# Hybrid encoder trunk on one core: 1/rms of a phase's tokens by ScalarE's square root, VectorE's reciprocal and one Newton step

## Chip, core and metric

The kernel runs on one core of a Trainium2 chip. The core has TensorE (PE in the profile; its weight loads are PEld), VectorE (DVE), ScalarE (ACT), GpSimd (POOL) and SyncE (SP), each with its own instruction stream that runs in order; they wait for each other by semaphores. The metric is the device time of one execution in microseconds, as the median over runs.

## The reference

Two layers, each a token mixer (gated delta rule, pooling, retention) and a SwiGLU feed-forward network, on 512 tokens of 1024 channels in float32. Each of the two halves of a layer is wrapped in two RMS norms, one ahead of it and one behind it:

```python
def rms_norm(x, w):
    xf = x.astype(jnp.float32)
    y = xf * lax.rsqrt(jnp.mean(xf * xf, axis=-1, keepdims=True) + RMS_EPS) * w.astype(jnp.float32)
    return y.astype(x.dtype)

def reference(x, mix_pre_norm, ..., ffn_down):
    for l in range(DEPTH):
        h = rms_norm(x, mix_pre_norm[l])
        m = hybrid_mixer(h, w_in[l], ...)
        x = x + rms_norm(m, mix_post_norm[l])
        h = rms_norm(x, ffn_pre_norm[l])
        x = x + rms_norm(swiglu(h, ffn_gate[l], ffn_up[l], ffn_down[l]), ffn_post_norm[l])
    return x
```

The mixer's gates of the delta rule use a sigmoid (`beta`) and exponentials (the decay `g`); the other gates are sigmoids.

## The kernel before

Activations lie with channels on the 128 partitions and the 512 tokens along the free dimension, in eight tiles of 128x512. Every float32 product is made of three matmuls of rounded operands (`mm3`, lines 225 to 228): each operand is split into a high part, which ScalarE rounds, and a low part, which VectorE gets by subtracting (`split`, `split1`, lines 230 to 237). The names are `hh`/`hl` for the normed input, `wh`/`wl` for weights, `oh`/`ol` for a branch's input, `ah`/`al` for the feed-forward activation. Products go to PSUM tiles `pp` and `cx`, small ones to `fx`.

A norm takes these steps. ScalarE squares the tiles (`sq`, line 286), GpSimd adds them (`sqa`, line 293), TensorE sums over the partitions against a column of ones (`rms_tok`, line 271), so that each token's sum stands on a partition, in 2 or 4 columns. VectorE takes 1/sqrt there (`rms_tok` line 273 and `rsqrt`, lines 239 to 264: a start value from the exponent bits, then two polynomial steps; ten instructions in all, `rsv`, `rsi`, `rsy`, `rsa`, `rsb`). TensorE spreads the result over the partitions (`spread`, line 279), and others multiply by it. `rsqrt` is called in the mixer too, for other norms.

`mean_square` (line 320) is called 15 times. `begin` (line 361) calls it once at the very start, for the first layer's input. `hand_over` (line 399) joins two halves of the network, and runs four times. It makes the last output blocks of one half in two token halves of 256 (`produce`), norms each half (`accs`), adds it to the residual `xt` and splits the new operand (`step`: lines 332, 333, 232, 233, 286), and starts the first four products of the next half: three in `cx` banks (`group_step`) and a fourth in a `pp` bank (`alone`). The next half's own norm (`pre`) is spread while that runs (lines 463 to 469) and behind it (474 to 476). At the end of the kernel (lines 412 to 431) `hand_over` only finishes: the last spread is followed by lines 341 and 342 and the output's DMA.

At the start of a mixer `token_gates` (line 527) works out `beta` (sigmoid, 551), `e` (exp of the tokens' decay, 563), `ea` (exp of a layer constant, 565) and, through a chain of small VectorE instructions, `g`, whose sums TensorE makes at line 591. At the same time the pooling branch's operands `oh` are split (line 1014, which calls `split`) for the first branch product `pp<-oh,wh`.

ScalarE's functions come from tables, and where the table that is loaded lacks a function, an ACT_TABLE_LOAD stands ahead of the instruction. Copies and squares stand behind any of the loads. Before the change 24 loads stand on ScalarE: the first at the start, the others where sigmoid and exp take turns, eleven in the first mixer and twelve in the second.

The order of each engine's stream is set by a scheduler from the program order, priorities (`tc.high_priority`, lines 210 and 219) and its own estimate of each instruction. `tc.issue_after(ins)` keeps what is traced in its block behind `ins` on its engine. So an edit in one helper moves instructions elsewhere.

Of the kernel before, what the change touches and what calls it, by code (L numbers as in the profile page):

```python
# [9 lines left out]
F32 = mybir.dt.float32  # L10
F32R = mybir.dt.float32r
I32 = mybir.dt.int32
AF = mybir.ActivationFunctionType
ALU = mybir.AluOpType
# [121 lines left out]
def tile_hybrid(ctx: ExitStack, tc: tile.TileContext, x_in, consts, rot, rmask, vecs, wab, wi, wpl, wbr, wo, wgu, wd, out):  # L136
# [18 lines left out]
    one = cpool.tile([P, 1], F32, tag="one", name="one")  # L155
    V.memset(one0, 1.0)
    A.activation(out=one, in_=one0, func=AF.Copy)

    def cm(n):
        return kc[:, n * P : (n + 1) * P]  # L160
# [18 lines left out]
    def nm(s):  # L179
        uid[0] += 1  # L180
        return f"{s}_{uid[0]}"

    def psum(pool, tag):
        return pool.tile([P, S], F32, tag=tag, name=nm(tag))
# [10 lines left out]
    def psum_o():  # L195
        return psum(fx, "fx")
# [42 lines left out]
    def rsqrt(pool, v, n):  # L239

        def new(tag, bufs=2, dt=F32):
            return pool.tile([P, n], dt, tag=f"{tag}{n}", bufs=bufs, name=nm(tag))

        i = new("rsi", dt=I32)
        V.tensor_scalar(out=i, in0=v.bitcast(I32), scalar1=1, scalar2=None, op0=ALU.logical_shift_right)
        y = new("rsy", 4)
        V.tensor_scalar(out=y.bitcast(I32), in0=i, scalar1=-1.0, scalar2=1597463007.0, op0=ALU.mult, op1=ALU.add)
        a = new("rsa")  # L250
        V.tensor_tensor(out=a, in0=y, in1=y, op=ALU.mult)
        b = new("rsb")
        V.tensor_tensor(out=b, in0=a, in1=v, op=ALU.mult)
        a = new("rsa")
        V.scalar_tensor_tensor(out=a, in0=b, scalar=-3.4181694869972654, in1=b, op0=ALU.add, op1=ALU.mult)
        z = new("rsy", 4)
        V.scalar_tensor_tensor(out=z, in0=a, scalar=5.24672026895501, in1=y, op0=ALU.add, op1=ALU.mult)
        a = new("rsa")
        V.scalar_tensor_tensor(out=a, in0=z, scalar=-0.0625, in1=z, op0=ALU.mult, op1=ALU.mult)
        b = new("rsb")  # L260
        V.tensor_tensor(out=b, in0=a, in1=v, op=ALU.mult)
        y = new("rsy", 4)
        V.scalar_tensor_tensor(out=y, in0=b, scalar=1.5, in1=z, op0=ALU.add, op1=ALU.mult)
        return y

    def rms_tok(sqs, ps, scale, eps):

        n = sqs[0].shape[1] // P
        for t in range(n):
            for i, sq in enumerate(sqs):  # L270
                T.matmul(ps[:, t : t + 1], lhsT=sq[:, ts(t)], rhs=one, start=i == 0, stop=i == len(sqs) - 1)  # L271
        v = hpool.tile([P, n], F32, tag=f"rsv{n}", bufs=2, name=nm("rsv"))
        V.tensor_scalar(out=v, in0=ps[:, :n], scalar1=8 * scale, scalar2=8 * eps, op0=ALU.mult, op1=ALU.add)
        return rsqrt(hpool, v, n)

    def spread(r, ps):

# [41 lines left out]

    def mean_square(acc):  # L320

        return rms_tok(acc, psum_o(), 1.0 / D, RMS_EPS)

    def spread_new(r):
        ps = psum_f()
# [26 lines left out]
    def rest(gen):  # L352
        for _ in gen:
            pass
# [5 lines left out]

    def begin(pool, l, v0, srcs):

        z = pool.tile([P, S // 2], F32, tag="z", name="z")
        V.memset(z, 0.0)
        ps = psum_f()
        for _ in range(4):
            T.matmul(ps[:, 0 : S // 2], lhsT=z[:, 0:P], rhs=z, start=True, stop=True)
        n = 3 * P
        xs = [pool.tile([P, S], F32, tag="xt", bufs=KT, name=nm("xt")) for _ in range(KT)]
        raw, wh, wl = (pool.tile([P, KT * n], t, tag=a, name=a) for a, t in (("w", F32), ("wh", F32R), ("wl", F32R)))  # L370
        for k in range(KT):
            nc.sync.dma_start(out=xs[k], in_=x_in[k])
            nc.sync.dma_start(out=raw[:, k * n : (k + 1) * n], in_=srcs[0][k])
        nc.sync.dma_start(out=ident, in_=consts[:, 0:P])
        hs, rb = operands()
        pss = [psum_c() for _ in range(3)]
        for k in range(KT):
            split(xs[k], vec[:, l, v0 + k : v0 + k + 1], *hs[k])
            high = nc.cur_bb.bb.instructions[-2]
            sl = slice(k * n, (k + 1) * n)  # L380
            split1(raw[:, sl], wh[:, sl], wl[:, sl])
            for j, ps in enumerate(pss):
                at = slice(k * n + j * P, k * n + (j + 1) * P)
                mm3(ps, (wh[:, at], wl[:, at]), hs[k], k == 0, k == KT - 1)
        f = last_block(srcs[3], hs, pss)
        with tc.issue_after(high):
            acc = accumulate(pool, None, xs)
        some(f, 2)
        r = mean_square(acc)
        rest(f)  # L390
        f = last_block(srcs[4], hs, pss)
        some(f, 1)
        A.activation(out=rb, in_=spread_new(r), func=AF.Copy)
        last["rb"] = nc.cur_bb.bb.instructions[-1]
        rest(f)
        nc.sync.dma_start(out=kc, in_=consts[:, P:])
        return x_in, hs, rb, pss

    def hand_over(pool, l, v_post, xs, pairs, ms, produce, nxt):
# [2 lines left out]
        w = vec[:, l, v_post : v_post + KT]  # L402
        h0, h1 = HALVES
        accs = {}
        rest(produce(0, accs))
        p1 = produce(1, accs)
        some(p1, 2)
# [96 lines left out]
    def mixer(l, xd, hs, rb, firsts):  # L504
# [22 lines left out]
        def token_gates():  # L527
# [34 lines left out]
            e = tiny("e")  # L562
            A.activation(out=e, in_=nab, func=AF.Exp)
            ea = tiny("ea")
            A.activation(out=ea, in_=vec[:, l, V_ALOG : V_ALOG + 16], func=AF.Exp)
            den = tiny("den")
            V.tensor_scalar(out=den, in0=e, scalar1=2.0, scalar2=None, op0=ALU.add)
            V.reciprocal(out=den, in_=den)
# [873 lines left out]
```

## Time and profile before

| | |
|---|---|
| median of 3 runs | 1843.85 us (1843.64 to 1846.25) |
| the profiled execution | 1842.82 us |
| its span, first to last instruction | 1841.0 us |
| mean granted TensorE clock | 0.997 |
| PE busy | 1814.3 us (99%) |
| PEld busy | 1536.9 us (83%) |
| DVE busy | 1052.1 us (57%) |
| ACT busy | 711.3 us (39%) |
| POOL busy | 373.3 us (20%) |

A matmul's duration in the trace overlaps that of the next one, so TensorE's rate is read from the distance of starts: 256 columns follow each other by 0.12 us, 512 columns by 0.23 us. A wait in square brackets names what ended the idle time. Idle time of TensorE is what the kernel can still lose or win; idle time of the others costs nothing by itself.

### The profile page before, as it was taken

How to read it: one execution, taken by the hardware profiler on the slowest of the kernel's cores; microseconds unless marked ns; L12 is line 12 of the kernel's file. 1: busy time of each engine (PE TensorE's matmuls, PEld its weight loads, DVE VectorE, ACT ScalarE, POOL GpSimd, SP SyncE). 2: the span in 40 equal slices, each digit the busy share in tenths (PEclk: the TensorE clock that was granted, in tenths of full speed). 3: DMA queues.
4: the chain of work that ended last, by engine and by line, in shares of the span. 5: the costliest groups of instructions: out<-in, count | busy, mean ns of one | idle time of the engine just before them, and what ended most of it. 6: DMA issues, size and time to landing. Idle time of an engine off the chain costs nothing.

```text
span 1841.0 us, 25237 instructions
## 1 busy us (share of the span) xinstructions
PE 1814.3 (99%) x9528; PEld 1536.9 (83%) x9528; DVE 1052.1 (57%) x1998; ACT 711.3 (39%) x1272; POOL 373.3 (20%) x350
## 2 busy tenths in 40 slices
PE   9999999999999999999999999999999999999997
PEld 7777888888898888888987778888888988888887
DVE  7778766664457432444687787666644574324443
ACT  5553333333344333333445533333334443333331
POOL 2040211011233210221210402110121332102212
PEclk9999999999999999999999999999999999999998
DMA  5312212124325222222232221221343252323221
GB/s 186 118 59 94 75 61 83 58 81 137 103 81 183 101 94 100 95 94 102 81 127 94 89 82 64 72 72 47 103 138 117 73 178 92 103 92 100 95 92 47
DMA packets 65850, 177.74 MB, mean 97 GB/s; under 512 B 15424, under 2 KB 19648, under 8 KB 65728
## 3 DMA queue, kind: packets, MB, share of 16 engines
q1 hardware_dynamic: 58800, 173.04, 28.0%
q10 hardware_dynamic: 6928, 3.08, 0.6%
q8 instruction: 75, 1.23, 0.3%
q14 instruction: 47, 0.39, 0.1%
HBM read 167.18 MB, written 8.39 MB: 95 GB/s over the span
## 4 chain that ended last, share of the span: by engine, by line
PE 90%; DVE 7%; ACT 1%; issue 1%; DMA 0%; SPq 0%; POOL 0%; ACTq 0%; DVEq 0%
PE pp L226 26%; PE pp L228 26%; PE pp L227 26%; DVE ct L641 1%; DVE wl L237 1%; PE cx L227 1%; PE cx L226 1%; PE cx L228 1%; PE cx L849 1%; PE cx L932 1%; PE fx L271 1%; PE cx L942 1%; PE cx L834 1%; PE cx L521 1%; PE fx L521 1%
## 5 line engine op out<-in xcount | busy, mean ns | idle before, releaser
L226 PE MATMUL pp<-hh,wh 128*128 128x512 f32 (+1 forms) x1592 | 626.2, 393 | 0.0
L228 PE MATMUL pp<-hh,wl 128*128 128x512 f32 (+1 forms) x1592 | 616.9, 387 | 0.0
L227 PE MATMUL pp<-hl,wh 128*128 128x512 f32 (+1 forms) x1592 | 615.4, 387 | 0.0
L236 ACT ACTIVATE wh<-raw 128x512 fp32r<-128x512 f32 x570 | 355.0, 628 | 665.6 <-PE pp L227 609.8
L237 DVE TENSOR_TENSOR wl<-raw,wh 128x512 fp32r<-128x512 f32 x570 | 417.6, 738 | 264.4 <-ACT wh L236 254.7
L228 PEld LDWEIGHTS pp<-hh,wl 128*128 128x128 f32 x1592 | 299.0, 188 | 61.9 <-issue 0.7
L226 PEld LDWEIGHTS pp<-hh,wh 128*128 128x128 f32 x1592 | 299.3, 188 | 59.8 <-issue 1.0
L227 PEld LDWEIGHTS pp<-hl,wh 128*128 128x128 f32 x1592 | 299.4, 188 | 57.4
L226 PE MATMUL pp<-ah,wh 128*128 128x512 f32 (+1 forms) x376 | 134.7, 358 | 0.0
L227 PE MATMUL pp<-al,wh 128*128 128x512 f32 (+1 forms) x376 | 134.4, 357 | 0.0
L228 PE MATMUL pp<-ah,wl 128*128 128x512 f32 (+1 forms) x376 | 134.4, 357 | 0.0
L1309 POOL TENSOR_TENSOR gs<-gt,sg 128x512 f32<-128x512 f32 x44 | 56.7, 1288 | 314.0 <-ACT sg L1307 314.0
L1314 POOL TENSOR_TENSOR a<-gs,ut 128x512 f32<-128x512 f32 x44 | 70.5, 1602 | 130.1 <-DVE ut L1312 129.6
L293 POOL TENSOR_TENSOR sqa<-sqa,sq 128x256 f32<-128x256 f32 (+1 forms) x73 | 68.7, 941 | 107.4 <-ACT sq L286 88.1
L226 PEld LDWEIGHTS pp<-ah,wh 128*128 128x128 f32 x376 | 71.0, 189 | 10.5
L227 PEld LDWEIGHTS pp<-al,wh 128*128 128x128 f32 x376 | 71.1, 189 | 10.3
L228 PEld LDWEIGHTS pp<-ah,wl 128*128 128x128 f32 x376 | 71.0, 189 | 10.3
L237 DVE TENSOR_TENSOR al<-a,ah 128x512 fp32r<-128x512 f32 x44 | 31.3, 711 | 77.7 <-ACT ah L236 77.4
L226 PE MATMUL pp<-yh,wh 128*128 128x256 f32 (+1 forms) x224 | 67.1, 300 | 0.0
L228 PE MATMUL pp<-yh,wl 128*128 128x256 f32 (+1 forms) x224 | 66.8, 298 | 0.0
L227 PE MATMUL pp<-yl,wh 128*128 128x256 f32 (+1 forms) x224 | 66.8, 298 | 0.0
L1036 POOL TENSOR_TENSOR y<-y,ft 128x512 f32<-128x512 f32 x16 | 26.5, 1653 | 189.6 <-DVE ft L1035 173.1
(327 smaller groups left out, 2468.0 us busy)
## 6 DMA issues: line engine op xcount, KB each, us to landing
raw<-in_wi_dram SPq DMA_DIRECT2D x117, 512.0 KB
raw<-in_wgu_dram SPq DMA_DIRECT2D x88, 512.0 KB
raw<-in_wd_dram SPq DMA_DIRECT2D x44, 512.0 KB
raw<-in_wbr_dram SPq DMA_DIRECT2D x24, 512.0 KB
raw<-in_wo_dram SPq DMA_DIRECT2D x16, 512.0 KB
xd<-xt SPq DMA_DIRECT2D x24, 256.0 KB
xt<-xd SPq DMA_DIRECT2D x24, 256.0 KB
xt<-in_x_dram SPq DMA_DIRECT2D x16, 256.0 KB
```

The costliest lines, as they stand in the source:

```text
L226: T.matmul(ps, lhsT=w[0], rhs=m[0], start=start, stop=False)
L227: T.matmul(ps, lhsT=w[0], rhs=m[1], start=False, stop=False)
L228: T.matmul(ps, lhsT=w[1], rhs=m[0], start=False, stop=stop)
L236: A.activation(out=hi, in_=src, func=AF.Copy)
L237: V.tensor_tensor(out=lo, in0=src, in1=hi.bitcast(F32), op=ALU.subtract)
L271: T.matmul(ps[:, t : t + 1], lhsT=sq[:, ts(t)], rhs=one, start=i == 0, stop=i == len(sqs) - 1)
L293: G.tensor_tensor(out=t, in0=acc[0], in1=acc[1], op=ALU.add)
L521: T.transpose(ps[:, ts(t)], src[:, ts(t)], ident)
L641: V.scalar_tensor_tensor(out=a2, in0=u[:, j : j + S], scalar=tap(j), in1=a, op0=ALU.mult, op1=ALU.add)
L1036: G.tensor_tensor(out=ys[n], in0=ys[n], in1=t, op=ALU.add)
L1309: G.tensor_tensor(out=gs, in0=gt, in1=sg, op=ALU.mult)
L1314: G.tensor_tensor(out=a, in0=gs, in1=ut, op=ALU.mult)
```

## The change

`rms_tok` no longer calls `rsqrt`. ScalarE takes sqrt(scale*x + eps) from PSUM, VectorE takes the same sum's plain value `v`, the reciprocal of the root, and one Newton step of three instructions. That is one instruction on ScalarE and five on VectorE in place of ten on VectorE, 15 times.

Sqrt has a table of its own. `root_table` runs a Sqrt on one column so that the load stands early: at the start of `begin`, and at the start of each `hand_over`, there behind the ScalarE instruction that was traced last (`behind`). In `token_gates` the exponential `ea` is tied behind `e`. The other calls of `rsqrt` stay.

```diff
+    eps = cpool.tile([P, 1], F32, tag="eps", name="eps")
+    V.memset(eps, RMS_EPS)
...
+    def behind(engine):
+        return tc.issue_after(next(i for i in reversed(nc.cur_bb.bb.instructions) if i.engine == engine))
...
-    def rms_tok(sqs, ps, scale, eps):
+    def rms_tok(sqs, ps, scale):
...
-        v = hpool.tile([P, n], F32, tag=f"rsv{n}", bufs=2, name=nm("rsv"))
-        V.tensor_scalar(out=v, in0=ps[:, :n], scalar1=8 * scale, scalar2=8 * eps, op0=ALU.mult, op1=ALU.add)
-        return rsqrt(hpool, v, n)
+        q, v, y, z = (new(t) for t in ("rsq", "rsv", "rsy", "rsz"))
+        a, b = new("rsa", 1), new("rsb", 1)
+        A.activation(out=q, in_=ps[:, :n], func=AF.Sqrt, scale=scale, bias=eps)
+        V.tensor_scalar(out=v, in0=ps[:, :n], scalar1=scale, scalar2=RMS_EPS, op0=ALU.mult, op1=ALU.add)
+        V.reciprocal(out=y, in_=q)
+        V.scalar_tensor_tensor(out=a, in0=y, scalar=-0.5, in1=y, op0=ALU.mult, op1=ALU.mult)
+        V.tensor_tensor(out=b, in0=a, in1=v, op=ALU.mult)
+        V.scalar_tensor_tensor(out=z, in0=b, scalar=1.5, in1=y, op0=ALU.add, op1=ALU.mult)
+        return z
+
+    def root_table():
+        t = hpool.tile([P, 1], F32, tag="rst", name=nm("rst"))
+        A.activation(out=t, in_=one0, func=AF.Sqrt)
...
     def begin(pool, l, v0, srcs):
+        root_table()
...
     def hand_over(pool, l, v_post, xs, pairs, ms, produce, nxt):
...
+        with behind(A.engine):
+            root_table()
         rest(produce(0, accs))
...
-            A.activation(out=ea, in_=vec[:, l, V_ALOG : V_ALOG + 16], func=AF.Exp)
+            with behind(A.engine):
+                A.activation(out=ea, in_=vec[:, l, V_ALOG : V_ALOG + 16], func=AF.Exp)
```

The scheduler then sets other orders. Three places follow; line numbers of the changed kernel are larger by about 26 (split is 238 and 239, spread 301, `ea` 591, `oh` 238).

ScalarE at the very start: `one` is the column of ones, `hh` the first operand's high part. Before:

```order
L157 ACT_TABLE_LOAD
L157 ACTIVATE one<-one_79 128x1
L232 ACTIVATE hh_121<-xt_93,vec 128x512
L236 ACTIVATE wh<-w 128x384
L232 ACTIVATE hh_123<-xt_94,vec 128x512
```

After:

```order
L157 ACT_TABLE_LOAD
L157 ACTIVATE one<-one_79 128x1
L296 ACT_TABLE_LOAD
L296 ACTIVATE rst_88<-one_79 128x1
L238 ACTIVATE hh_125<-xt_97,vec 128x512
```

A load and a one-column root stand ahead of the first operand.

TensorE in the first `hand_over`, where `pre[0]`'s result `rsy` (after: `rsz`) is spread; `cx` are the three grouped products of the next half, `pp` the fourth. Before:

```order
L228 MATMUL cx_5223<-hh_5005,wl_5242 128x256
L226 MATMUL pp_5226<-hh_4999,wh_5358 128x256
L227 MATMUL pp_5226<-hl_5000,wh_5358 128x256
L228 MATMUL pp_5226<-hh_4999,wl_5359 128x256
L226 MATMUL cx_5221<-hh_5007,wh_5275 128x256
L226 MATMUL cx_5222<-hh_5007,wh_5282 128x256
L226 MATMUL cx_5223<-hh_5007,wh_5289 128x256
L226 MATMUL pp_5226<-hh_5001,wh_5358 128x256
L227 MATMUL pp_5226<-hl_5002,wh_5358 128x256
L279 MATMUL fx_5539<-ident,rsy_5429 128x128 x2
L227 MATMUL cx_5221<-hl_5008,wh_5275 128x256
```

After:

```order
L234 MATMUL cx_5213<-hh_4995,wl_5232 128x256
L232 MATMUL cx_5211<-hh_4997,wh_5265 128x256
L232 MATMUL cx_5212<-hh_4997,wh_5272 128x256
L232 MATMUL cx_5213<-hh_4997,wh_5279 128x256
L301 MATMUL fx_5513<-ident,rsz_5396 128x128
L233 MATMUL cx_5211<-hl_4998,wh_5265 128x256
```

The spread now comes in two parts, the first five `pp` matmuls earlier. The `pp` product is moved to the rear: 19 of its 24 matmuls follow the last `cx` matmul, where 12 did. The other two middle `hand_over`s read the same.

ScalarE in the second layer's `token_gates`: `beta` and the two `ft` are sigmoids, `e` and `ea` exponentials, `ct` and `oh` need no table of their own. Before (`ea`, with a load of its own, stands seven rows ahead of this piece):

```order
L551 ACT_TABLE_LOAD
L551 ACTIVATE beta_9032<-fx_9017 128x16
L975 ACTIVATE ft_8938<-ft_8936 128x512
L236 ACTIVATE wh_9303<-raw_9284 128x512
L975 ACTIVATE ft_8977<-ft_8975 128x512
L232 ACTIVATE oh_9088<-fx_9086,vec 128x512
L563 ACT_TABLE_LOAD
L563 ACTIVATE e_9038<-nab_9036 128x16
L638 ACTIVATE ct_9054<-ft_9051,vec 128x512
L232 ACTIVATE oh_9100<-fx_9098,vec 128x512
```

After:

```order
L576 ACT_TABLE_LOAD
L576 ACTIVATE beta_8968<-fx_8953 128x16
L1001 ACTIVATE ft_8874<-ft_8872 128x512
L242 ACTIVATE wh_9239<-raw_9220 128x512
L1001 ACTIVATE ft_8913<-ft_8911 128x512
L588 ACT_TABLE_LOAD
L588 ACTIVATE e_8974<-nab_8972 128x16
L591 ACTIVATE ea_8976<-vec 128x16
L664 ACTIVATE ct_8990<-ft_8987,vec 128x512
L238 ACTIVATE oh_9024<-fx_9022,vec 128x512
L238 ACTIVATE oh_9036<-fx_9034,vec 128x512
```

The first `oh` moves from ahead of the load to behind `ct`. In the first layer it already stood there before the change (load, `e`, `ct`, `oh`); there only `ea` comes in between `e` and `ct`.

In all, ScalarE has 30 table loads after the change: one more at the start, one more in each of the four `hand_over`s, one more at the first sigmoid of each of the two feed-forward networks, and one less for `ea`. None stands directly ahead of a norm's root.

## Rows read from the trace of the kernel before

**Rows 1.** The page: engine totals, and the costliest group on ScalarE.

```profile
PE 1814.3 (99%) x9528; PEld 1536.9 (83%) x9528; DVE 1052.1 (57%) x1998; ACT 711.3 (39%) x1272; POOL 373.3 (20%) x350
...
L236 ACT ACTIVATE wh<-raw 128x512 fp32r<-128x512 f32 x570 | 355.0, 628 | 665.6 <-PE pp L227 609.8
```

**Rows 2.** TensorE's waits: total us, times, longest us.

```profile
PE fx L279 <- DVE rsy L263: 4.0, 4, 2.1
PE pp L226 <- ACT oh L232: 1.9, 1, 1.9
```

**Rows 3.** Timeline of the end: start us, duration, instruction, [idle before].

```profile
1829.32 0.16 DVE L273 TENSOR_SCALAR rsv<-fx 128x2 f32<-128x2 f32 x1 [1.37 <-PE fx L271]
...
1831.09 0.16 DVE L263 SCALAR_TENSOR_TENSOR rsy<-rsb,rsy 128x2 f32<-128x2 f32 x1
...
1831.39 1.19 PE L279 MATMUL fx<-ident,rsy 128*128 128x128 f32 x4 [2.12 <-DVE rsy L263]
```

**Rows 4.** Groups by line: the reciprocal that the kernel has (busy us, mean ns).

```profile
L568 DVE RECIPROCAL den<-den 128x16 f32<-128x16 f32 x2 | 0.5, 253 | 0.1
```

**Rows 5.** Timeline of the first hand-over, around the spread of `pre[0]`.

```profile
560.15 0.16 DVE L273 TENSOR_SCALAR rsv<-fx 128x2 f32<-128x2 f32 x1 [0.61 <-PE fx L271]
...
562.88 0.70 DVE L255 SCALAR_TENSOR_TENSOR rsa<-rsb 128x2 f32<-128x2 f32 x1
...
564.37 0.28 PE L226 MATMUL pp<-hh,wh 128*128 128x256 f32 x1
...
565.44 0.70 DVE L263 SCALAR_TENSOR_TENSOR rsy<-rsb,rsy 128x2 f32<-128x2 f32 x1
...
566.29 0.68 PE L279 MATMUL fx<-ident,rsy 128*128 128x128 f32 x4 [0.62 <-DVE rsy L263]
...
570.93 0.48 DVE L233 SCALAR_TENSOR_TENSOR hl<-xt,vec,hh 128x256 fp32r<-128x256 f32 x1 [0.58 <-ACT hh L232]
...
573.61 0.28 PE L228 MATMUL pp<-hh,wl 128*128 128x256 f32 x1
573.73 0.40 PE L226 MATMUL pp<-hh,wh 128*128 128x512 f32 x1
```

**Rows 6.** Timeline of the first layer's token gates.

```profile
42.93 0.39 PE L538 MATMUL fx<-hh,abw 128*128 128x512 f32 x1
...
52.85 1.28 ACT L563 ACT_TABLE_LOAD   x1
...
54.15 0.22 ACT L563 ACTIVATE e<-nab 128x16 f32<-128x16 f32 x1
54.27 0.70 ACT L638 ACTIVATE ct<-ft,vec 128x512 f32<-128x512 f32 x1
...
55.60 0.50 PE L226 MATMUL pp<-oh,wh 128*128 128x512 f32 x1 [1.88 <-ACT oh L232]
...
95.96 0.63 PE L723 MATMUL cx<-ident,wq 128*128 128x128 f32 x4 [0.32 <-DVE wq L653]
```

**Rows 7.** Timeline of the second layer's token gates.

```profile
956.68 0.39 PE L538 MATMUL fx<-hh,abw 128*128 128x512 f32 x1
...
966.16 0.61 ACT L975 ACTIVATE ft<-ft 128x512 f32<-128x512 f32 x1
...
966.68 0.67 ACT L232 ACTIVATE oh<-fx,vec 128x512 fp32r<-128x512 f32 x1
...
967.40 0.50 PE L226 MATMUL pp<-oh,wh 128*128 128x512 f32 x1
...
1007.83 0.63 PE L723 MATMUL cx<-ident,wq 128*128 128x128 f32 x4 [0.31 <-DVE wq L653]
```

**Rows 8.** Timeline of the start.

```profile
2.54 0.20 ACT L157 ACTIVATE one<-one 128x1 f32<-128x1 f32 x1
...
3.89 0.72 ACT L232 ACTIVATE hh<-xt,vec 128x512 fp32r<-128x512 f32 x1 [1.15 <-DMA vec<-in_vecs_dram]
...
5.07 1.22 PE L226 MATMUL cx<-hh,wh 128*128 128x512 f32 x2
```

More of the change, by code (lines that the diff above doesn't have):

```diff
@@ L271, in rms_tok, with new @@
                 T.matmul(ps[:, t : t + 1], lhsT=sq[:, ts(t)], rhs=one, start=i == 0, stop=i == len(sqs) - 1)
-        v = hpool.tile([P, n], F32, tag=f"rsv{n}", bufs=2, name=nm("rsv"))
-        V.tensor_scalar(out=v, in0=ps[:, :n], scalar1=8 * scale, scalar2=8 * eps, op0=ALU.mult, op1=ALU.add)
-        return rsqrt(hpool, v, n)
+        def new(tag, bufs=2):
+            return hpool.tile([P, n], F32, tag=f"{tag}{n}", bufs=bufs, name=nm(tag))
+        q, v, y, z = (new(t) for t in ("rsq", "rsv", "rsy", "rsz"))
[10 more added lines that the diff above has]
+        A.activation(out=t, in_=one0, func=AF.Sqrt)
     def spread(r, ps):
@@ L320, in mean_square @@
     def mean_square(acc):
-        return rms_tok(acc, psum_o(), 1.0 / D, RMS_EPS)
+        return rms_tok(acc, psum_o(), 1.0 / D)
     def spread_new(r):
```

## Prediction

> **What bounds the kernel now.** I read the engine totals first, then TensorE's waits, then the timeline around each place where the change or its new order touches TensorE. TensorE is busy for 1814.3 of 1841.0 us, and ScalarE spends 610 us waiting for TensorE to free weight buffers [rows 1]. So removing VectorE work or adding ScalarE work in the middle of a product is worth nothing; only TensorE's waits count. The ones that end on the norm's last instruction are four, 4.0 us together [rows 2]: 2.12 us at the very end [rows 3], and one of about 0.62 us in each middle `hand_over` (one is shown [rows 5]; 4.0 less 2.12 leaves 1.9 for the three). The norms' other 11 spreads make TensorE wait for nothing that the profile names; there the shorter chain is hidden already. So what can be won directly is under 4 us, 0.2% of the kernel. The second thing to read is what the new order does to waits that have nothing to do with the norm: the largest of them is 1.88 us behind ScalarE's `oh` [rows 2, 6].
>
> **The change part by part.** The sum is made against the profiled execution: 1842.82 us, of which 1841.0 are span. The median of the runs is 1843.85, so 1.03 us above it; I carry the difference over to the median unchanged.
>
> (a) The end. All is exposed: TensorE has nothing else. Before, ten dependent instructions run from 1829.32 to 1831.25, one each 0.195 us (1829.32 to 1831.09 is nine steps) [rows 3]. After, ScalarE's root starts when VectorE's `rsv` started, at 1829.32. No Sqrt stands in the trace; the nearest row is an exponential of 16 columns, 0.22 us [rows 6], taken for it (two columns against sixteen could only shorten it). The hop to VectorE lies between the 0.03 from one VectorE step to the next and the 0.14 from VectorE's last step to TensorE (1831.25 to 1831.39); 0.05 is taken, near the lower end since TensorE's start is the longer one. The plain value `v` runs beside it. The reciprocal of 16 columns takes 0.25 [rows 4], 0.09 more than a two-column step, so its step is 0.20 to 0.29. Then two steps of 0.195 and a last instruction of 0.16: 0.22 + 0.05 + 0.24 + 0.39 + 0.16 = 1.06 us in place of 1.93. That is **-0.85 us** (-0.75 to -0.95). What follows is the same work, shifted.
>
> (b) Three `hand_over`s, at `pre[0]`. Here the ten small instructions stand between large ones on VectorE, which is itself the late engine: it delivers the last low operand `hl` at 571.41, and TensorE is finished with the stage at 573.73 [rows 5]. From 564.37 TensorE has 60 matmuls of 0.12 us (36 `cx`, 24 `pp`) and the spread, 0.5 (its record of 0.68 less the 0.16 by which a matmul's record outlasts its slot): 7.7 us of work, and it takes 9.36, so 1.7 us are lost, far more than the 0.62 of the named wait. The removal helps VectorE in two ways. `rsv` no longer makes it stand idle 0.61 us for TensorE, since two large instructions now go ahead of it; and the two of the ten that took 0.70 us instead of 0.15 are gone, 1.1 us [rows 5]. So the last `hl` may come 1.7 us earlier, at 569.7. But the fourth product, which filled gaps, is now at the rear: behind the last `hl` stand 6 `cx` and 19 `pp` matmuls, 25 x 0.12 = 3.0 us, plus 0.1 for the start, where 2.3 stood. 569.7 + 3.1 = 572.8 instead of 573.73: **-0.9 us each, -2.7 in all**. One end is TensorE without any wait, 564.37 + 7.7 = 572.1: -1.6 each. The other is that another VectorE instruction takes the 0.70 and the last `hl` comes no earlier: 571.41 + 3.1 = 574.5, +0.8 each. I stay in the middle.
>
> (c) Second layer's token gates. Before, the first `oh` stands on ScalarE ahead of the load for `e`, starts at 966.68 and TensorE's branch product follows at 967.40 without a named wait [rows 7]. After, load, `e`, `ea` and `ct` are ahead of it. From the end of the sigmoid `ft` at 966.77: 1.28 for the load, 0.02, 0.12 for `e` and 0.12 for `ea` (starts of `e` and `ct` are 0.12 apart [rows 6]), 0.62 for `ct`; `oh` starts at 968.93 and ends at 969.6. TensorE, in order, waits from 967.4: +2.2 us. Whether a wait here is swallowed later is shown by the first layer, which has that order already and the 1.88 us wait. From the first `abw` matmul to the fourth transposition at line 723 TensorE has the same list of matmuls in both layers; it takes 53.03 us in the first and 51.15 in the second [rows 6, 7]. The difference is 1.88: the wait is paid in full. So **+2.1 us** (1.7 to 2.5).
>
> (d) First layer's token gates: `ea` comes between `e` and `ct`, ahead of the `oh` that TensorE waits for: **+0.1 us**. Its place at the start is emptied, but that was idle time.
>
> (e) The start. The new load and root stand ahead of the first `hh`, which starts at 3.89 when its data is there. `one` ends at 2.74 [rows 8]; plus 1.28 and 0.1 to 0.2 gives 4.12 to 4.24: **+0.3 us**. TensorE's first real matmul at 5.07 waits for this and TensorE has no pause to win it back.
>
> (f) At nothing: the other loads. In the `hand_over`s and at the feed-forward network's first sigmoids ScalarE is 1.28 us later, beside 610 us of waiting [rows 1]; weight splits run many matmuls ahead. If that cover failed, a load would cost TensorE up to 1.28 us, six times. In `begin` two DMA issues now stand behind the root, 5 us later; their data is used by TensorE at 42.93 [rows 6].
>
> Sum: -0.85 - 2.7 + 2.1 + 0.1 + 0.3 = **-1.05 us**: 1841.8 beside the profiled 1842.82, and 1842.8 as a median.
>
> [...] In rows, the load takes 1.28 us and the next instruction follows 0.02 us later (52.85, 54.15) [rows 6]. [...]
>
> **The rivals.**
>
> *Slower: the filler is missed.* In the three `hand_over`s VectorE stays late, because GpSimd's additions run beside it and the 0.70 us fall on another instruction. For it: two of ten were hit by chance of position, not by their kind; against it: 0.61 us of pure idling goes in any case. It decides at 570.7: if the last `hl` is ready later than that (on the old time scale), the new order loses. Price +0.8 each: -0.85 + 2.4 + 2.1 + 0.1 + 0.3 = +4.05, 1847.9.
>
> *Faster: the wait at `oh` does not come, and the stage runs full.* If the second layer's sigmoid `ft`, which waits behind a weight split, comes earlier, the load is over before `oh` is needed, and (c) falls; with (b) at its end of -1.6 each the sum is -0.85 - 4.8 + 0.4 = -5.25, 1838.6. Against it: ScalarE's splits wait for buffers that TensorE itself frees [rows 1].
>
> [...]
>
> *It does not do what it says.* The roots could find another table loaded and load again, 1.28 us in the chain at the end and in the stages: (a) turns to +0.4 and the sum to about +0.2 or more, 1844.1. The listing shows no load ahead of a root, so this has nearly nothing.
>
> **How the numbers follow.** The forecast, with everything within its bounds, has 0.66 and runs from 1840.5 to 1845. The missed filler has 0.12, half of it complete in all three stages; the faster rival 0.12, mostly in part (one of its two conditions: -0.85 - 4.8 + 2.1 + 0.4 = -3.15 or -0.85 - 2.7 + 0.4 = -3.15, near 1840.7); the slower switch 0.07, the last one 0.03. The likeliest is 1842.8. A measurement of this kernel can tell about 0.2%, 3.7 us, from no change. Below 1840.2 lie most of the faster rival and a tail of the forecast: 0.11. Above 1847.5 lies half of the slower one and a little more: 0.07. The rest, 0.82, is no change that can be told. The range of 8 in 10 leaves out the complete rivals at both ends: 1839.8 to 1846.
>
> **What would show it.** In the profile of the changed kernel: at the end, root to last Newton step in about 1.06 us and a wait of TensorE near 1.25 instead of 2.12; at the three `pre[0]` spreads no wait, and the first 512-column matmul of the fifth product 8.1 to 9 us after the stage's first `pp` slot instead of 9.36; a new wait of TensorE on ScalarE's `oh` of about 2 us near 967, beside the old one of 2.0; the first matmul at 5.4. Wrong would be a wait of TensorE on weights behind a load, or a stage in which the last `hl` is no earlier.

## The result, and the profile after

The changed kernel takes 1872.21 us as a median of four runs, against 1845.01 for the kernel before in the same comparison: a ratio of 1.0146, 95% interval 1.0129 to 1.0164. That is 27 us slower, far outside the range that was given. Nothing in the forecast was of that size, so the first question is where 29 us of span (1870.3 in place of 1841.0) lie.

The first line of the page of the changed kernel answers to the one in [rows 1]:

```profile
PE 1845.7 (99%) x9528; PEld 1534.8 (82%) x9528; DVE 1043.4 (56%) x1924; ACT 723.8 (39%) x1298; POOL 370.3 (20%) x350
```

TensorE runs the same 9528 matmuls, at the same share of the span, and is busy for 31.4 us more. So it is not waiting; its work takes longer. TensorE's waits (total us, times, longest us) say the same, next to [rows 2]:

```profile
PE pp L232 <- ACT oh L238: 3.8, 2, 2.2
PE cx L797 <- DVE wq L679: 2.9, 4, 1.1
PE cx L233 <- DVE hl L239: 2.4, 3, 0.8
PE fx L1137 <- DVE vc L1118: 1.8, 2, 1.0
PE fx L301 <- DVE rsz L290: 1.3, 1, 1.3
```

The four waits on the norm are one, as intended. The others are the old ones with other sizes: `oh` has 3.8 us in place of 1.9, and two more rows of before compare with the second and third row above:

```profile
PE cx L771 <- DVE wq L653: 4.1, 6, 1.4
PE cx L227 <- DVE hl L233: 0.9, 3, 0.3
```

Together all of TensorE's idle time fell from 26.7 to 24.6 us (span less busy time). What changed is the pace. The timeline gives it best in the feed-forward network, where TensorE runs 528 matmuls of `hh` and `hl` without a pause between two stretches of `ah`. The first and the last of them, before:

```profile
732.95 0.39 PE L226 MATMUL pp<-hh,wh 128*128 128x512 f32 x1
...
852.40 0.39 PE L228 MATMUL pp<-hh,wl 128*128 128x512 f32 x1
852.63 0.39 PE L226 MATMUL pp<-ah,wh 128*128 128x512 f32 x1
```

and after:

```profile
742.34 0.40 PE L232 MATMUL pp<-hh,wh 128*128 128x512 f32 x1
...
865.30 0.40 PE L234 MATMUL pp<-hh,wl 128*128 128x512 f32 x1
865.54 0.39 PE L232 MATMUL pp<-ah,wh 128*128 128x512 f32 x1
```

119.45 us over 527 steps are 226.7 ns from start to start; 122.96 us are 233.3 ns. The records themselves are 0.39 and 0.40 us long in both, so a column of durations hardly shows it; the distance of the starts does. The clock is granted in full in both (1.00 over each of the two stretches). Below I call that distance the slot, and take it in ns from the start times in the trace.

In such stretches the delay against the kernel before grows by 0.8 us with every 120 matmuls of 512 columns, in both layers; over stretches of 256 columns it shrinks, by 0.1 to 0.4 with as many. It has nothing to do with the places where the norm stands. What differs everywhere is where the operands lie in SBUF. The diff adds two tiles of 4 bytes, each with 32 bytes of room: `eps` ahead of the weights' tiles and `rst` ahead of `hh`; and it allocates fewer small tiles for the root, 128 bytes less. From the compiled programs:

| first address of | before | after |
|---|---|---|
| weights `wh` | 36032 | 36064 |
| `hh` of the norm's output | 68800 | 68864 |
| `ah` of the feed-forward network | 124864 | 124800 |
| `yh` of the mixer's output | 174016 | 173952 |
| `oh` of the branches | 183936 | 183872 |

The tiles are multiples of 512 bytes apart among themselves, so each moving operand has one distance to the stationary one, modulo 256 bytes. Before, it is 0 for 5818 of the matmuls with 512 columns and 192 for the 384 of `oh` and `ol`. After, it is 32 for `hh`, 160 for `ah` and `yh`, 96 for `oh`, 128 for 104 products of the first layer, and 0 for no more than two of the matmuls with 512 columns. And the trace of before had the slow slot already: the products of `oh` and `ol` took 233.1 ns a slot there, beside 227.3 for those at 0.

So theory 1: a slot of 512 columns is short where moving and stationary operand lie a multiple of 256 bytes apart. Rivals: the roots and loads slow TensorE everywhere (theory 2); TensorE reads weights slowly that do not begin at a multiple of 64 bytes (theory 3).

### The profile page after: what moved, and what is told of

It reads as the page before. It is cut to its first block, busy times and chain, and to the rows that moved or that the text cites. A ratio compares the mean times of both kernels' runs of the same rounds, so it can differ in the third digit from the quotient of the medians.

```text
span 1870.3 us, 25181 instructions
## 1 busy us (share of the span) xinstructions
PE 1845.7 (99%) x9528; PEld 1534.8 (82%) x9528; DVE 1043.4 (56%) x1924; ACT 723.8 (39%) x1298; POOL 370.3 (20%) x350
## 4 chain that ended last, share of the span: by engine, by line
PE 91%; DVE 6%; ACT 1%; issue 1%; DMA 0%; SPq 0%; POOL 0%; ACTq 0%; DVEq 0%
PE pp L232 26%; PE pp L234 26%; PE pp L233 26%; DVE ct L667 1%; PE cx L233 1%; PE cx L232 1%; PE cx L234 1%; PE cx L875 1%; PE cx L958 1%; PE cx L968 1%; PE cx L860 1%; DVE xt L355 1%; PE cx L546 1%; PE fx L277 1%; PE fx L546 1%
## 5 line engine op out<-in xcount | busy, mean ns | idle before, releaser
L232 PE MATMUL pp<-hh,wh 128*128 128x512 f32 (+1 forms) x1592 | 634.0, 398 | 0.0
L234 PE MATMUL pp<-hh,wl 128*128 128x512 f32 (+1 forms) x1592 | 624.4, 392 | 0.0
L233 PE MATMUL pp<-hl,wh 128*128 128x512 f32 (+1 forms) x1592 | 623.5, 392 | 0.0
L315 POOL TENSOR_TENSOR sqa<-sqa,sq 128x256 f32<-128x256 f32 (+1 forms) x73 | 63.9, 875 | 107.2 <-ACT sq L308 85.1
```

The source lines that it names most:

```text
L232: T.matmul(ps, lhsT=w[0], rhs=m[0], start=start, stop=False)
L233: T.matmul(ps, lhsT=w[0], rhs=m[1], start=False, stop=False)
L234: T.matmul(ps, lhsT=w[1], rhs=m[0], start=False, stop=stop)
L315: G.tensor_tensor(out=t, in0=acc[0], in1=acc[1], op=ALU.add)
```

## Experiments: where the 29 us come from

**The changed kernel with the old addresses.** The two small tiles go into unused bytes of a tile that is there, and 128 bytes are left free behind the norm's small tiles. No instruction moves.

```diff
-    one0 = cpool.tile([P, 1], F32, tag="one0", name="one0")
+    small = cpool.tile([P, 8], F32, tag="one0", name="one0")
+    one0, eps, rst = (small[:, i : i + 1] for i in range(3))
...
-    eps = cpool.tile([P, 1], F32, tag="eps", name="eps")
...
+        hpool.tile([P, 32], F32, tag="pad", name=nm("pad"))
         q, v, y, z = (new(t) for t in ("rsq", "rsv", "rsy", "rsz"))
...
-        t = hpool.tile([P, 1], F32, tag="rst", name=nm("rst"))
-        A.activation(out=t, in_=one0, func=AF.Sqrt)
+        A.activation(out=rst, in_=one0, func=AF.Sqrt)
```

> The changed kernel, same instructions in the same order on every engine, but every tile that it shares with the kernel before (the norm's own small tiles excepted) at the SBUF address that it had there: the constant for the root's bias and the root table's target take unused bytes of the tile of ones, and 128 bytes are left free behind the norm's small tiles. Theory 1 (addresses): TensorE's 512-column matmuls follow each other every 227 ns where the moving operand and the stationary operand lie a multiple of 256 bytes apart, and every 233 ns where they don't; in the changed kernel none of the large products has that distance. Then the slots are 227 ns again in the second feed-forward product, 31.6 us of the 29.3 us come back (5818 slots x 5.9 ns less 1300 slots of 256 columns x 2.1 ns), and the span is near 1838.7, the time 1841 to 1843. Theory 2 (the roots and table loads, or the shorter instruction streams, slow TensorE everywhere): nothing changes, 1872. What is left against the kernel before shows the terms of my sum: -0.8 at the end, +0.25 at the start, +2 and a lower clock behind it at the second layer's token gates, and the three hand-overs.

1843.48 us, ratio to the kernel before 1.0001 (0.9992 to 1.001), just above the 1841 to 1843 that were expected; the profiled span is 1841.6. The slots are 226.7 ns in the stretch above, and TensorE is busy 1814.2 us. The first of two stretches that are used again below, one inside the products of `hh`, in the changed kernel and then in this run (columns: the stretch, then busy us and instructions of PE, PEld, DVE, ACT and POOL, the granted clock, DMA share, GB/s):

```profile
590.00:670.00 80.00, 80.00 (x344) 64.27 (x343) 37.36 (x53) 27.35 (x45) 24.43 (x17) 1.00 0.31 99
590.00:670.00 80.00, 80.00 (x354) 66.24 (x354) 35.52 (x54) 28.36 (x47) 23.06 (x16) 1.00 0.32 100
```

Theory 2 falls: the same roots and loads, in the same order, cost TensorE nothing there. The span gives back 28.7 us, less than the 31.5 that TensorE's busy time does, since TensorE idles 2.8 us more: `wq` at line 797 took 2.9 us with the long slots and takes 4.1 with the short ones, and the waits on `cv` at line 546 are back with 1.3 us.

**The kernel before, everything 32 bytes further.** One constant more ahead of the weights, which nobody reads:

```diff
     A.activation(out=one, in_=one0, func=AF.Copy)
+    eps = cpool.tile([P, 1], F32, tag="eps", name="eps")
+    V.memset(eps, RMS_EPS)
```

> The kernel before with one 4-byte constant more among its constants, set once and read by nobody: all tiles behind the constants lie 32 bytes further, and their distances from each other stay. Theory 1 (distance of the two operands): no change, 1843.5 to 1845.5. Rival, theory 3 (TensorE reads weights slowly that don't begin at a multiple of 64 bytes, as in the changed kernel): the weights' tiles begin 32 bytes off, +27 us, 1872.

1844.04 us, ratio 1.0002 (0.9993 to 1.0011). The weights begin 32 bytes off a multiple of 64 here, as in the changed kernel, and the slots stay at 226.7:

```profile
590.00:670.00 80.00, 80.00 (x355) 66.24 (x354) 36.34 (x56) 27.80 (x46) 23.13 (x16) 1.00 0.31 99
```

Theory 3 falls, and with it the suspicion against `eps`: what all tiles share costs nothing.

**The kernel before, operands 32 bytes further than the weights.** The same constant, one pool later:

```diff
     A.activation(out=one, in_=one0, func=AF.Copy)
+    eps = hpool.tile([P, 1], F32, tag="eps", name="eps")
+    V.memset(eps, RMS_EPS)
```

> The kernel before with the same 4-byte constant, but behind the weights' tiles and ahead of the operands': weights stay where they were, everything behind lies 32 bytes further. Theory 1: the distance is 32 bytes for 5712 of the 512-column matmuls and 1312 of the 256-column ones: +5.9 ns x 5712 - 3.1 ns x 1312 = +29.6 us, about 1873.5. Theory 3: weights still begin at multiples of 64 bytes, no change, 1844. That neither roots nor loads nor the norm have to do with it is shown by this run alone, if it is slow.

1870.47 us where 1873.5 was expected, ratio 1.0149 (1.0135 to 1.0163). The kernel before, with its norm untouched and one idle constant more, is as slow as the changed kernel. Two stretches of this run, one inside the products of `hh` and one inside those of `ah` (columns as above):

```profile
590.00:670.00 80.00, 80.00 (x344) 64.26 (x344) 37.42 (x55) 28.00 (x47) 26.67 (x19) 1.00 0.33 108
688.00:728.00 40.00, 40.00 (x173) 32.11 (x173) 10.65 (x16) 11.69 (x20) 0.00 (x0) 1.00 0.32 98
```

The kernel before gets more matmuls into the same time, at the same clock:

```profile
590.00:670.00 80.00, 80.00 (x355) 66.25 (x354) 35.46 (x54) 27.99 (x46) 22.33 (x16) 1.00 0.30 99
688.00:728.00 40.00, 40.00 (x179) 33.10 (x178) 9.79 (x15) 12.73 (x21) 0.00 (x0) 1.00 0.28 93
```

355 against 344 in 80 us is the whole finding in one pair of rows.

**Which of the tiles.** The changed kernel with `rst` alone moved away; `eps` keeps its tile.

```diff
-    one0 = cpool.tile([P, 1], F32, tag="one0", name="one0")
+    small = cpool.tile([P, 8], F32, tag="one0", name="one0")
+    one0, rst = (small[:, i : i + 1] for i in range(2))
...
-        t = hpool.tile([P, 1], F32, tag="rst", name=nm("rst"))
-        A.activation(out=t, in_=one0, func=AF.Sqrt)
+        A.activation(out=rst, in_=one0, func=AF.Sqrt)
```

> The changed kernel with one tile moved: the 4-byte target of the root table lies in unused bytes of the tile of ones in place of a tile of its own ahead of hh. The constant eps keeps its tile, so weights and operands both lie 32 bytes further than before; hh and hl are at a multiple of 256 from the weights again (4634 slots), and the mixers', tails' and feed-forward tiles are 128 off (1184 slots of 512 columns at 232 in place of 227, +5.8 us). About 1848 to 1849: that one tile is then worth 24 of the 29 us, and eps nothing. If eps's 32 bytes were the cause, 1872.

1849.76 us, ratio 1.0032 (1.0022 to 1.0041): as expected, a little above. `hh` is back at a multiple of 256 from the weights and fast; `ah` is 128 off and slow, in one and the same run:

```profile
590.00:670.00 80.00, 80.00 (x354) 66.25 (x353) 36.83 (x56) 27.98 (x46) 21.96 (x17) 1.00 0.31 99
688.00:728.00 40.00, 40.00 (x173) 32.16 (x172) 10.23 (x15) 12.17 (x21) 0.00 (x0) 1.00 0.30 100
```

So the 4-byte target of the root table made some 22 of the 27 us, and the small tiles of the norm that are no longer there the rest.

**Is it all or nothing?** `hh` and `hl` 64 bytes off, in the changed kernel with the old addresses:

```diff
     def operands():
+        hpool.tile([P, 16], F32, tag="gap", name=nm("gap"))
...
-        hpool.tile([P, 32], F32, tag="pad", name=nm("pad"))
+        hpool.tile([P, 16], F32, tag="pad", name=nm("pad"))
```

> As the changed kernel in the old layout, but hh and hl lie 64 bytes further; everything behind them stays. 64 is the one step of 32 within 256 that no run has had. If only multiples of 256 are fast: 4742 slots of 233 ns, +26 us against the run in the old layout, about 1869, and the feed-forward network's second product (ah, not moved) stays at 227 ns beside the first at 233. If multiples of 64 were enough: no change, 1843.5.

1848.55 us in one run, where 1869 was expected: a miss. The slots of `hh` are 228.9 ns, between the two; those of `ah`, which was not moved, 226.8.

```profile
590.00:670.00 80.00, 80.00 (x351) 65.71 (x350) 36.30 (x56) 27.65 (x46) 21.90 (x15) 1.00 0.31 99
688.00:728.00 40.00, 40.00 (x178) 33.11 (x178) 10.39 (x15) 12.68 (x21) 0.00 (x0) 1.00 0.33 103
```

The distance grades the slot; 0 is the best of the eight steps of 32, and 64 is nearer to it than to the others. Mean slots, for `hh` and `ah` with 512 columns over the long stretches of the feed-forward network:

| distance modulo 256 | 512 columns, ns | 256 columns, ns | operands, run |
|---|---|---|---|
| 0 | 226.7 | 119.9 | `hh`, `ah`, before |
| 32 | 233.3 | 116.8 to 117.4 | `hh`, after and operands 32 off; `yh`, placed |
| 64 | 228.9; 230.5 | 117.8 | `hh`, operands 64 off; `oh`, `rst` alone moved |
| 96 | 233.3 | | `oh`, after |
| 128 | 233.3 | 118.6 | `ah`, `rst` alone moved |
| 160 | 234.2 | 119.1 | `ah`, after |
| 192 | 233.1 | | `oh`, before |
| 224 | 233.1 | | `oh`, operands 32 off |

With 256 columns it is the other way round: the distance of 0 is the slowest, by 0.8 to 3.1 ns.

**Own weights, or the next ones?** The next matmul's weights are loaded while one runs: in the 119.45 us of `hh` and `hl` above, before, all 527 weight loads, 0.19 us each, lie within a matmul's record, and the one for the matmul of 740.21 starts at 739.98 with the matmul ahead of it. To see which distance counts, the low weights alone were put 32 bytes further, in the kernel before:

```diff
-                wh, wl = self.home("wh"), self.home("wl")
+                wh = self.home("wh")
+                wpool.tile([P, 8], F32, tag="gap", name=nm("gap"))
+                wl = self.home("wl")
```

> The kernel before with 32 bytes left free between the weights' high tiles (which stay) and their low tiles; the low tiles and all that follows lie 32 bytes further. The three matmuls of a product come in the order hh x wh, hl x wh, hh x wl; hh and hl lie 32 bytes off from wh and at a multiple of 256 from wl. Theory 1a (what counts is the distance between the moving operand and the weights that are loaded meanwhile for the next matmul): hh x wh 233 ns, hl x wh (wl loads) 227, hh x wl (wh loads) 233. Theory 1b (the matmul's own weights count): 233, 233, 227. Either way two of three slots are slow: 3800 x 5.9 ns less 880 x 3 ns, +20 us, about 1864.

1869.42 us in one run, where 1864 was expected, and neither pattern: 235.2, 232.9 and 231.3 ns for `hh` with `wh`, `hl` with `wh` and `hh` with `wl`. No slot of the three is short, though each theory had one. Together they are 699 ns, 233.1 each: one product with two matmuls off and one in place is as slow as one with all three off. What happens inside a slot stays open, and so does the question whether the own weights or the next ones count.

A second sign that a slot does not go by its own distance alone stands in the trace with `hh` 64 bytes off. There 192 products of `os` (line 902 of the kernel before, a branch's gated output) stand in groups of twelve behind `hh`. Their operands lie where they lay in the changed kernel with the old addresses, at a multiple of 256, and there all of them take 226 or 227 ns; here they take 230.6 on average. In most groups the first ten slots lie between 224 and 237 ns, and the last two are back at 226 to 228. So the table holds for long runs of products with one distance, and where the operands change the pace can take some products to settle. What carries over from one product to the next, no run here shows.

## Experiments: the terms of the sum

With the addresses out of the way, the changed kernel in the old layout shows the terms of the forecast one by one against the kernel before.

**The token gates.** In that run the second layer's token gates take 55.05 us from the first `abw` matmul (955.36) to the fourth transposition (1010.41), against 51.15 before [rows 7]: +3.9 us. ScalarE and then TensorE:

```profile
965.47 1.28 ACT L588 ACT_TABLE_LOAD   x1
966.77 0.22 ACT L588 ACTIVATE e<-nab 128x16 f32<-128x16 f32 x1
966.89 0.20 ACT L591 ACTIVATE ea<-vec 128x16 f32<-128x16 f32 x1
966.99 0.71 ACT L664 ACTIVATE ct<-ft,vec 128x512 f32<-128x512 f32 x1
967.61 1.25 ACT L238 ACTIVATE oh<-fx,vec 128x512 fp32r<-128x512 f32 x2
...
968.33 0.50 PE L232 MATMUL pp<-oh,wh 128*128 128x512 f32 x1 [2.17 <-ACT oh L238]
```

The wait is there as worked out, 2.17 us. But it is followed by something else. Stretches behind it (columns as above; the granted clock is the third number from the end):

```profile
968.00:969.00 1.00, 0.68 (x3) 0.59 (x4) 1.00 (x3) 0.85 (x2) 0.00 (x0) 1.00 0.58 238
969.00:970.00 1.00, 1.00 (x5) 0.79 (x4) 1.00 (x4) 0.00 (x0) 0.00 (x0) 0.75 0.00 0
970.00:971.00 1.00, 1.00 (x3) 0.34 (x1) 1.00 (x3) 0.00 (x0) 0.00 (x0) 0.50 0.02 8
```

After TensorE had stood idle for these 2.17 us, the granted clock was 0.75 and then 0.50. In the run with `hh` 64 bytes off the same wait of 2.17 us was not followed by such a fall (1.00 from 968 to 976), and the same stretch took 53.44 us. So the wait cost 2.2 us, as forecast, and the fall behind it another 1.6. The fall does not belong to this wait alone. In the kernel before with everything 32 bytes further, the first layer's wait is as long as in [rows 6], and in that profile the clock fell to 0.50 behind it:

```profile
55.46 0.52 PE L228 MATMUL pp<-oh,wh 128*128 128x512 f32 x1 [1.90 <-ACT oh L234]
...
56.00:57.00 1.00, 1.00 (x3) 0.78 (x3) 1.00 (x3) 0.00 (x0) 0.00 (x0) 0.50 0.49 197
```

That stage took 54.67 us there, against 53.03 in the kernel before, where the clock stayed at 1.00 behind the wait (55 to 59). Is it the order behind `ea` that makes the wait? One part of the change undone, all else as in the changed kernel with the old addresses:

```diff
-            with behind(A.engine):
+            if True:
                 A.activation(out=ea, in_=vec[:, l, V_ALOG : V_ALOG + 16], func=AF.Exp)
```

> The changed kernel in the old layout, with one part of the change undone: ea is not held behind e any more. It goes back to the place where it stood, with a table load of its own in each mixer, and in the second layer one oh stands ahead of e's load again. If the order behind ea is what made the second layer's token gates 3.9 us longer (55.05 in place of 51.15 us, a wait of 2.17 us and a lower clock behind it), they are about 51.2 us again and the time is 1839.5 to 1840.5. Rival (the roots' loads or the earlier start of that stage make the wait): 55 us again and 1843.5.

1838.93 us, ratio 0.9974 (0.9962 to 0.9985), a little under what was expected. In the second layer one `oh` stands ahead of the load again, TensorE does not wait for it, and the stretch takes 50.73 us (955.28 to 1006.01):

```profile
965.28 0.67 ACT L238 ACTIVATE oh<-fx,vec 128x512 fp32r<-128x512 f32 x1
965.97 1.28 ACT L588 ACT_TABLE_LOAD   x1
...
966.00 0.50 PE L232 MATMUL pp<-oh,wh 128*128 128x512 f32 x1
...
967.26 0.21 ACT L588 ACTIVATE e<-nab 128x16 f32<-128x16 f32 x1
```

The table load that the change saves at `ea` was free; the order that it brought was not.

**oh ahead of e.** A higher priority for the branch's operands, on the changed kernel and on the kernel before:

```diff
-            operand("p", gi, lambda a, b: split(ps, vec[:, l, V_PS + gi : V_PS + gi + 1], a, b))
+            with tc.high_priority(offset=AHEAD):
+                operand("p", gi, lambda a, b: split(ps, vec[:, l, V_PS + gi : V_PS + gi + 1], a, b))
```

> As the run with the changed kernel in the old layout, but with a higher priority for the pooling branch's operands, so that two of the oh stand on ScalarE ahead of the table load for e in both layers. My step (c): the waits for oh of 1.9 and 2.2 us go, and with them the fall of the clock behind the second one (about 2 us): 4 to 6 us less than that run, 1836 to 1838. Rival (the wait is swallowed by work that is late for another reason, or the branch's first product, which now stands earlier on TensorE, waits for its weights): within 1 us of that run.

> The kernel before, with the higher priority for the pooling branch's operands and nothing else: what the roots are worth by themselves, where both kernels have the old addresses and oh ahead of e. By the terms read in the trace of the changed kernel in the old layout (end -0.8, hand-overs -0.55 each, start +0.25) the run with the roots should be about 2.2 us the shorter one, so this one 1842 to 1843.5. If the roots are worth nothing beside what hides them: equal, 1840.6.

The changed kernel in the old layout comes to 1840.62 us, ratio 0.9984 (0.9976 to 0.9993), the kernel before to 1842.0, ratio 0.9995 (0.9986 to 1.0004). The first gains less than expected, since waits of 0.93 and 1.46 us on `oh` stay, now behind a product that stands earlier on TensorE. The difference of the two, 1.4 us by the medians where 2.2 was expected, is about what the roots are worth where neither addresses nor the order of `oh` stand between; the two intervals overlap, so its size is not certain.

**Placing on purpose.** If the distance counts, tiles can be put where it is best: 64 bytes ahead of `oh` bring it to a multiple of 256, 32 bytes ahead of `yh`, most of whose matmuls have 256 columns, take it off one.

```diff
+            tl("gap", 1, (P, 16))
             a, b = tl("oh", H, dt=F32R), tl("ol", H, dt=F32R)
...
+                tl("gap", 1, (P, 8))
                 a, b = tl("yh", KT, dt=F32R), tl("yl", KT, dt=F32R)
```

> As the run with oh first, and two placements more: 64 bytes ahead of oh and ol, which bring them to a multiple of 256 from the weights (384 slots of 512 columns, 233 to 227 ns: -2.3 us), and 32 bytes ahead of yh and yl, which take them off it (576 slots of 256 columns, 119.9 to 116.8: -1.8 us; 96 of 512 columns, +0.6 us). -3.5 us against that run: 1837. If the distance mattered only for hh and ah: no change, 1840.6.

> The changed kernel in the old layout, ea undone as before, and the two placements (oh and ol 64 bytes further, at a multiple of 256 from the weights; yh and yl 32 bytes further, off it). The order is that of the run with ea undone, so the difference is the slots alone: 384 x (233.1 - 228.8) = -1.65 us, 576 x (119.9 - 117.4) = -1.4, 96 x 6 = +0.6: -2.5 us, 1836.5. If the placements gave nothing: 1838.9.

> The same and oh first. In the second layer's token gates the order behind ea alone took 50.7 us and oh first 52.6, in the first layer 52.7 and 52.2: if the two add up as stages, oh first loses 1.4 us on top of ea undone, 1838. If oh first without ea in the way is better than either, below 1836.

With `oh` first, the two gaps bring 1840.62 to 1837.53 us, ratio 0.997 (0.9958 to 0.9982): -3.1 where -3.5 was expected. The slots of `oh` are 228.2 ns, not quite 227, and here too the mean hides two paces: in one group of twelve the first nine read 235, 233, 237, 224, 231, 235, 229, 232 and 231 ns, the last three 226, 227 and 227. Those of `yh` with 256 columns are 117.4. On the kernel with `ea` undone they bring 1838.93 to 1836.27, ratio 0.9957 (0.9943 to 0.9971): -2.7. All together, with `oh` first, 1835.91, ratio 0.9955 (0.9943 to 0.9967), where 1838 was expected if the stages add up; the second layer's gates take 51.1 us there. That is the fastest kernel of this study, 7.6 us under the kernel before by the medians: the roots, without the move of `ea`, and the tiles at chosen distances. The last two cannot be told apart.

## Why the prediction was wrong, and where it was right

**The step that failed** stands in its first paragraph: that only TensorE's waits count. The busy time of 1814.3 us was taken as a constant, and the change as what it does to instructions. The edit also does something to tiles: it adds `eps`, `rst`, `rsq` and `rsz`, drops `rsi` from the norm's pool and gives others there fewer buffers, and the pools lay out everything behind them anew. No term of the sum, no rival and no bound had that in it, so 27 us could not come out. The runs showed in its place that the same 9528 matmuls keep TensorE busy for 31.4 us more, since most slots of 512 columns are 233 to 234 ns long and no longer 227; one idle tile of 4 bytes does it to the kernel before (1870.47 us), and the old addresses undo it in the changed one (1843.48). It could have been seen: the addresses are in the compiled program, and the slow slots of `oh` were in the trace of before, a stretch of the same shape at another pace.

**The terms**, read in the changed kernel with the old addresses, whose profiled span is 0.6 us above the kernel before:

(a) The end: right. TensorE waits 1.30 us in place of the 2.12 of [rows 3], -0.82 against -0.85 forecast. In the changed kernel itself:

```profile
1859.34 0.26 ACT L285 ACTIVATE rsq<-fx,eps 128x2 f32<-128x2 f32 x1 [0.38 <-PE fx L277]
1859.63 0.16 DVE L286 TENSOR_SCALAR rsv<-fx 128x2 f32<-128x2 f32 x1 [1.66 <-ACT rsq L285]
1859.71 0.15 DVE L287 RECIPROCAL rsy<-rsq 128x2 f32<-128x2 f32 x1
...
1860.60 1.19 PE L301 MATMUL fx<-ident,rsz 128*128 128x128 f32 x4 [1.30 <-DVE rsz L290]
```

The root takes 0.26 us, the bound that stood for it was 0.22; `v` does not run beside it but right behind, at a cost of 0.08. The spread itself ran at a granted clock of 1.00 in the old layout (0.68 us) and of 0.50 in [rows 3] (1.19), which gave another 0.4 us that nobody forecast; in the changed kernel itself it ran at 0.50 again (1.19).

(b) The hand-overs: the sign and the mechanism right, the size off. From the first `cx` matmul of the second half to the first 512 columns the three take 13.20 to 13.22 us in place of 13.75: -0.55 each, -1.65 in all, where -0.9 each was taken. No wait for the spread is left, and the filler stands behind as the order showed. But the long VectorE steps went to others, the second part of the rival "the filler is missed":

```profile
560.38 0.70 DVE L355 SCALAR_TENSOR_TENSOR xt<-pt,vec,xt 128x256 f32<-128x256 f32 x1
...
562.27 1.35 DVE L355 SCALAR_TENSOR_TENSOR xt<-pt,vec,xt 128x256 f32<-128x256 f32 x2
...
569.33 0.48 DVE L239 SCALAR_TENSOR_TENSOR hl<-xt,vec,hh 128x256 fp32r<-128x256 f32 x1
```

The step of 0.70 us and the first of the two in the second row stand beside an addition of GpSimd (559.99 to 560.79 and 562.06 to 562.95), as the two long steps of before did (562.68 to 563.56 and from 565.21): that speaks for the reason which the rival gave, though no run here tests it. In the trace of before 8 of the 28 two-column steps at lines 255 and 263 lie beside an instruction of GpSimd and take 0.69 to 0.72 us, the other 20 take 0.16. The last `hl` is ready at 569.81, on the scale of before (this stage began 0.21 us sooner) at 570.02: later than the 569.7 that the sum used, earlier than the 570.7 from which the new order loses.

(c) The second layer's token gates: the wait right (2.17 against 2.1 to 2.2), its price mis-sized. It was priced by the first layer's wait, behind which the clock stayed at 1.00; behind this one the granted clock fell, in three of the four profiles with this order (to 0.50 in the changed kernel and in the old layout), and the term is +3.9 us. That the fall to 0.50 followed a wait of 1.90 us in the first layer too (54.67 us) shows that even there the price is not always the wait alone: in that profile the two stages differ by 3.5 us, and that they differ by just 1.88 in the one trace which the sum was read from was chance.

(d) The first layer's gates: 52.79 in place of 53.02, -0.23 where +0.1 was taken; the wait on `oh` is 1.65, not 1.88, and not longer.

(e) The start: +0.25 at the first product, forecast +0.3, of which 0.18 are left at the first `abw` matmul. In the changed kernel:

```profile
2.75 1.28 ACT L296 ACT_TABLE_LOAD   x1
4.04 0.20 ACT L296 ACTIVATE rst<-one 128x1 f32<-128x1 f32 x1
4.15 0.71 ACT L238 ACTIVATE hh<-xt,vec 128x512 fp32r<-128x512 f32 x1
...
5.32 1.22 PE L232 MATMUL cx<-hh,wh 128*128 128x512 f32 x2 [0.30 <-ACT wh L242]
```

The root follows the load by 0.01 us, and so does ScalarE's next instruction behind 28 of the other 29 loads, each of 1.28 us; behind one it waits 0.41 for TensorE's `cx` (line 617). The slower switch, with 0.07 of the chances, is shown by no run. A root that loads again is out as well: of the 30 loads none stands at line 285.

(f) The other loads: hidden, as forecast; no wait on weights came up beyond 0.3 us.

Together: -0.82 - 0.39 (the spread at the end) - 1.65 + 3.90 - 0.23 + 0.18 = +0.99, where the two spans differ by 0.6; the other 0.4 lie in the products between the gates and the next `hand_over` of both layers, which I did not take apart. So with the addresses held, the change is worth nothing as it stands (ratio 1.0001), where -1.05 us was forecast. That lies within the range, but (b) and (c) came out 2.9 us worse than the sum had them, and what made up for part of it (the clock at the end, (d), those products) was not forecast: that part is luck. Without the move of `ea` the change is worth 4.3 us by the medians.

## What to carry to other kernels

Before a diff is read for its instructions, read it for its tiles: a tile more or less ahead of others moves them all, and here one of 4 bytes moved TensorE's pace by 1.2% of the kernel. Compare the compiled addresses of before and after, and keep them where the question is what an edit does; a change timed with its addresses moved is two changes. A span that grows while the waits do not is the sign: compare the distance of matmul starts at one shape in the two traces before looking at any wait.

## What was not expected of the hardware

- The slot of a float32 matmul with 512 columns depends on the distance of moving and stationary operand in SBUF: 226.7 ns at a multiple of 256 bytes, 228.9 to 230.5 at 64, 233 to 234 at every other multiple of 32. With 256 columns it is 119.9 at 0 and 116.8 to 119.1 elsewhere. Moving all of them by 32 bytes together left it at 226.7 and the time at 1844.04 us, a ratio of 1.0002. These are means over runs of products with one distance; where the operands change, slots at a multiple of 256 took up to ten products to come down to 226 or 227 in four of the traces.
- The recorded weight loads do not show it: 188 ns in both kernels. Nor do the matmuls' own records, 0.39 and 0.40 us.
- One wait of TensorE of 2.17 us was followed by a fall of the granted clock in three profiles (to 0.50 in the changed kernel and in the old layout) and not in a fourth: the stage took 55.05 us in the old layout, 53.44 in the fourth; behind a wait of 1.90 us it fell in one profile and behind 1.88 us in another it did not.
